# A hybrid attention layer on one core: later loads for the compressed blocks' bias, second sums one a step, masks and a value load spread out

## The chip, the cores and the metric

The kernel runs on one core of a Trainium2 chip. The metric is the device time of one execution in microseconds (us), the median of several runs.

## The reference

One decoder layer works on x of 512 x 2048 in fp32. One combined projection h = x @ w_in (11808 columns) feeds two attentions side by side and two merge gates:

```
yA  = (FoX(q, k, v, f) * silu(zA)) @ w_a          8 heads of 128
yB  = (NSA(q, 3 pairs of k/v, gates) * silu(zB)) @ w_b   8 heads, 2 groups of keys and values
out = LayerNorm(alpha * x + (sigmoid(gA)*yA + sigmoid(gB)*yB) @ w_o)
```

FoX adds c_t - c_s to its causal logits, where c is the running sum of the log forget gates; c_t drops out in the softmax, so what is added is the row of -c, masked above the diagonal. NSA mixes three branches: 31 compressed blocks (32 positions each, every 16 positions, through a small two-layer net), selected blocks and a window. Every logit of NSA gets a bias from a table of 32 distances per head; for the compressed branch this is `cbias`, one value for each position and block, masked where the block isn't past.

## The kernel before

Each fp32 product is made of three products of 32-bit "r" numbers: both operands are split into a rounded part and the rest (`split`, lines 96 to 99: ScalarE writes the rounded part, VectorE subtracts), and `mm3` (line 106) multiplies high by high, high by low and low by high. In the trace the parts of a weight are `wh` and `wl`, those of x are `xs`.

The order of the work is written out by hand. A list of units (`units`) is walked by `stream`; unit n first emits the weight split of unit n+3 (`split_w`), whose four `wh` and `wl` buffers are reused in turn, and then its own products. A dense unit has four slices of the contraction, 12 products of 512 columns; after every second slice `tick()` lets each background job advance by one step. Jobs are Python generators, a `yield` ends a step. First come those in `active` in the order of joining (loads, biases, evacuations), then the head of the queue `tq` (transposes of probabilities and products with values) and of `sq` (logits and softmax). What a step emits stands at that place in the queue of its engine, and each engine runs its queue in order; an engine that has no wait can run far ahead of the step that TensorE has reached.

The stages, in order of time:

- the transposes of x and the first projections, to about 63 us;
- `pairs`, to 561.6 us: six jobs compute 512 x 1024 pieces of the projection by sums and differences of operands (Strassen's way), seven products in each job in the order T4, T1, B11, T2, B21, T3, B22. Each has 8 units of 6 products of 512 columns, with one step after each. After T3 `out2` (line 1066) adds its result to the kept sums `c5` and `c1`, two halves each, and evacuates the four sums to DRAM by ScalarE and SyncE (`keep`, lines 1172 and 1173);
- the FoX heads, from 561.6 us: per head projections of k and q (8 units, 16 steps), with the units of the block compression between those of heads 1 to 3 and 4 to 6. `attention_open` starts three jobs, in this order in `active`: `biases`, which runs `fox_bias` for each head (GpSimd loads the row of -c to all partitions as `cbr`, and writes four masked pieces `cbx`; two `cbx` buffers, freed by `fox_s`), `raw_load` (GpSimd loads the compression's input) and `block_bias` (line 691). The last makes `cbias` as needed on chip: per head a memset of the tile `cbT` on GpSimd, a load into it from the table `fwd_d` in DRAM, four steps of waiting, then four transposes on TensorE into a `pt` bank (line 701) and a copy to `cb` on VectorE. `cb` is first read in the NSA heads, at 874 us. The value of each head is loaded by GpSimd to `vT` (one buffer) and split by `v_load`;
- the NSA heads, from about 815 us: the same with `nsa_s` and `nsa_t`. The values of a group come through the same `vT` buffer in `nsa_v_load` (line 951), first "s" (selected), then "w" (window), each three steps after its load;
- the output products and the layer norm.

Of the kernel before, what the change touches and what calls it, by code (L numbers as in the profile page):

```python
# [12 lines left out]
F32 = mybir.dt.float32  # L13
F32R = mybir.dt.float32r
AF = mybir.ActivationFunctionType
ALU = mybir.AluOpType
# [4 lines left out]
P = 128  # L21
# [24 lines left out]
PW = P * NT * (NT + 1) // 2  # L46
# [17 lines left out]
def layer(ctx, tc, x, w_in, b_f, pos_k, pos_v, wk1, wk2, wv1, wv2, w_a, w_b, w_o, ln_g, ln_b, rel, onehot, out):  # L64
    nc = tc.nc

    def dram(t, off, ap):
        return bass.AP(tensor=t.tensor, offset=t.offset + off, ap=ap)
# [22 lines left out]
    def bank(tag, bufs):  # L91
        return ps.tile([P, S], F32, name=tag, tag=tag, bufs=bufs)

    def split(hi, lo, src, scale=None):

        if scale is None:
            nc.scalar.activation(hi, src, AF.Copy)  # L97
            nc.vector.tensor_tensor(lo, src, hi.bitcast(F32), op=ALU.subtract)  # L98
        else:
            nc.scalar.activation(hi, src, AF.Copy, scale=scale)  # L100
            nc.vector.scalar_tensor_tensor(lo, src, scale, hi.bitcast(F32), op0=ALU.mult, op1=ALU.subtract)
# [13 lines left out]
    active, copies = [], []  # L115
# [148 lines left out]
    def pool(name):  # L264
        return stage[name][1]
# [14 lines left out]
    def take_later(tag):  # L280
        while free[tag] == 0:
            yield
        free[tag] -= 1
# [41 lines left out]
    def zv_rows(c0):  # L325
        return dram(zvd[:], c0, [[2 * S, P], [P * 2 * S, NT], [1, DH]])
# [48 lines left out]
    def wait_for(*keys):  # L375
        while not all(k in done for k in keys):
            yield
# [119 lines left out]
    def fox_bias(h):  # L497

        c = pool("fox").tile([P, S], F32, name="cbr", tag="cbr", bufs=2)
        nc.gpsimd.dma_start(c, dram(negc_d, h * S, [[0, P], [1, S]]))  # L500
        m = pool("fox").tile([P, PW], F32, name="cbx", tag="cbx", bufs=2)
        for i in range(NT):
            n = (i + 1) * P
            nc.gpsimd.affine_select(m[:, OFF[i]:OFF[i] + n], c[:, :n], pattern=[[-1, n]], compare_op=ALU.is_ge,
                                    fill=NEG, base=i * P, channel_multiplier=1)
        return m

    def nsa_s(h, st):
        key, g = ("n", h), h // HPG
# [115 lines left out]
    def small(name, p, n):  # L625

        return pool("hd").tile([P, S], F32, name=name, tag="om", bufs=KT)[:p, :n]
# [62 lines left out]

    def block_bias():

        for h in range(H):
            t = small("cbT", CP, S)
            nc.gpsimd.memset(t, NEG)
            nc.gpsimd.dma_start(t[:NCMP], dram(fwd_d, h * NCMP * FL + 480, [[FL - CMP_STRIDE, NCMP], [1, S]]))
            for _ in range(4):
                yield
            m = bank("pt", 2)
            for i in range(NT):  # L700
                nc.tensor.transpose(m[:, i * CP:(i + 1) * CP], t[:, i * P:(i + 1) * P], ident[:CP, :CP])
            nc.vector.tensor_copy(cb[:, h], m[:, :NT * CP].rearrange("p (i c) -> p i c", c=CP))
            yield
# [56 lines left out]
    cbxs = {}  # L760

    def biases():
        for h in range(H):
            yield from take_later("cbx")
            cbxs[h] = fox_bias(h)
            yield
            done.add(("cbx", h))

    def fox_pre(h):
# [173 lines left out]
    def nsa_v_dst(br, g):  # L943
        def f():
            assert all(("t", ("n", h)) in done for h in range(g * HPG)), "values still held"
            t = pool("nsa").tile([P, 2, NT, DH], F32R, name="nv" + br, tag="nv" + br, bufs=1)
            vt[br, g] = (t[:, 0], t[:, 1])
            return t[:, 0].rearrange("p j d -> p (j d)"), t[:, 1].rearrange("p j d -> p (j d)")
        return f

    def nsa_v_load(br, g):

        yield from take_later("vT")
        v = pool("attn").tile([P, S], F32, name="vT", tag="vT", bufs=1)
        c0 = {"s": 0, "w": S}[br] + (2 + g) * DH
        nc.gpsimd.dma_start(v.rearrange("p (j d) -> p j d", d=DH), zv_rows(c0))
        if g:
            yield from wait_for(*(("t", ("n", h)) for h in range(g * HPG)))
        for _ in range(3):
            yield  # L960
        free["vT"] += 1
        hi, lo = nsa_v_dst(br, g)()
        split(hi, lo, v)
        done.add(("v", (br, g)))

    def nsa_kv(g):
        def pre():
            if g == 0:
                nsa_open()
            for br in "sw":  # L970
                active.append(nsa_v_load(br, g))

        proj(C_KS + g * DH, evac_k(("s", g), nsa_k_dst("s", g)), pre=pre)
        proj(C_KW + g * DH, evac_k(("w", g), nsa_k_dst("w", g)))


    HT = 2

    def pairs(jobs, ops, kh, ent):

        st = {}
# [26 lines left out]
        def one(j, w, ncols, r0, cols, width, evac):  # L1008
# [55 lines left out]
                    evac(i, cols[0], st[0][i][:, :width], None)  # L1064

            def out2(width=width, cols=cols, evac=evac):
                def job():
                    for i in range(HT):
                        c5 = st["c5"][:, i, :width]
                        nc.vector.tensor_tensor(c5, st[2][i][:, :width], c5, op=ALU.add)  # L1070
                        evac(HT + i, cols[1], c5, c5)
                    yield
                    for i in range(HT):
                        c1 = st["c1"][:, i, :width]
                        nc.vector.tensor_tensor(c1, st[2][i][:, :width], c1, op=ALU.add)
                        evac(i, cols[1], c1, c1)
                g = job()
                next(g)
                active.append(g)

            def out12(width=width, cols=cols, evac=evac):
                for i in range(HT):
# [3 lines left out]
            for op, acc, fresh, quad, after, post in (  # L1086
                    ("T4", 3, True, (1, 1), first_sum, no_post), ("T1", 1, True, "s", None, keep5),
                    ("B11", 0, True, (0, 0), both_sums, keep1), ("T2", 2, True, "s", "sum4", mix),
                    ("B21", 0, False, (1, 0), None, out11), ("T3", 2, False, "r", "rest", out2),
                    ("B22", 1, False, "s", None, out12)):  # L1090
                for k in range(kh):
# [113 lines left out]
    def attention_open():  # L1205
        drain(idle)
        close_pool("sr")
        close_pool("tw")
        open_pool("hd")
        open_pool("attn")  # L1210
        open_pool("fox")
        active.append(biases())
        active.append(raw_load())
        active.append(block_bias())
# [477 lines left out]
```

## Time and profile before

| | us |
|---|---|
| three runs | 1508.80, 1506.41, 1504.27 (median 1506.41) |
| the profiled execution | 1504.97 |
| its span | 1503.2 |
| TensorE busy in it | 1481.6 (99%) |
| VectorE, ScalarE, GpSimd busy | 874.8, 668.5, 235.2 |
| mean granted clock of TensorE | 0.997 |

The span runs from the first to the last instruction of one profiled execution; that execution's own time is 1.77 us longer. Busy times of the engines overlap. A granted clock of 1.00 is 2.4 GHz and of 0.50 is 1.2 GHz. In lists of instructions "PE" is TensorE's products, "PEld" its weight loads, "DVE" VectorE, "ACT" ScalarE, "POOL" GpSimd and "SP" SyncE.

### The profile page before, as it was taken

How to read it: one execution, taken by the hardware profiler on the slowest of the kernel's cores; microseconds unless marked ns; L12 is line 12 of the kernel's file. 1: busy time of each engine (PE TensorE's matmuls, PEld its weight loads, DVE VectorE, ACT ScalarE, POOL GpSimd, SP SyncE). 2: the span in 40 equal slices, each digit the busy share in tenths (PEclk: the TensorE clock that was granted, in tenths of full speed). 3: DMA queues.
4: the chain of work that ended last, by engine and by line, in shares of the span. 5: the costliest groups of instructions: out<-in, count | busy, mean ns of one | idle time of the engine just before them, and what ended most of it. 6: DMA issues, size and time to landing. Idle time of an engine off the chain costs nothing.

```text
span 1503.2 us, 19346 instructions
## 1 busy us (share of the span) xinstructions
PE 1481.6 (99%) x6905; PEld 1220.8 (81%) x6905; DVE 874.8 (58%) x1705; ACT 668.5 (44%) x1284; POOL 235.2 (16%) x375
## 2 busy tenths in 40 slices
PE   8999999999999998999999999999999999999998
PEld 6788888888888886888888888888888888888886
DVE  4666666666666662666664466646675444444455
ACT  6255655565656562454443344434453322322233
POOL 1211230101010206545500000000000100020001
PEclk9999999999999999999999999999999999999999
DMA  8678696868686855454533322232332433362336
GB/s 229 164 227 193 185 189 195 192 190 195 191 194 185 199 145 166 122 164 120 154 113 99 104 79 71 70 91 78 92 98 89 155 114 113 123 234 98 127 112 168
DMA packets 190703, 219.05 MB, mean 146 GB/s; under 512 B 13344, under 2 KB 125008, under 8 KB 190608
## 3 DMA queue, kind: packets, MB, share of 16 engines
q1 hardware_dynamic: 164720, 160.98, 35.2%
q0 software_dynamic: 25600, 56.32, 17.4%
q8 instruction: 54, 0.88, 0.2%
q10 hardware_dynamic: 288, 0.52, 0.1%
q14 instruction: 41, 0.34, 0.1%
HBM read 199.11 MB, written 22.32 MB: 147 GB/s over the span
## 4 chain that ended last, share of the span: by engine, by line
PE 94%; DVE 2%; DMA 1%; ACT 1%; issue 1%; POOL 1%; SPq 0%; POOLq 0%; ACTq 0%; DVEq 0%
PE d L106 45%; PE s L106 17%; PE o L106 10%; PE pt L106 10%; PE m L106 8%; PE pt L417 2%; DVE wl L98 1%; PE m L112 1%; PE o L112 1%; DMA vT<-zv_d 0%; PE d L1295 0%; ACT p L399 0%; DVE xs L98 0%; DMA cbT<-fwd_d 0%; DVE p L397 0%
## 5 line engine op out<-in xcount | busy, mean ns | idle before, releaser
L98 DVE TENSOR_TENSOR wl<-wr,wh 128x512 fp32r<-128x512 f32 x460 | 317.7, 696 | 292.4 <-ACT wh L97 287.6
L97 ACT ACTIVATE wh<-wr 128x512 fp32r<-128x512 f32 x460 | 286.8, 629 | 367.5 <-PE d L106 107.9
L106 PE MATMUL d<-xs,wh 128*128 128x512 f32 x1376 | 439.6, 400 | 0.5 <-ACT xs L97 0.3
L106 PEld LDWEIGHTS d<-xs,wh 128*128 128x128 f32 x1376 | 249.6, 190 | 47.9 <-DVE xs L98 1.6
L106 PE MATMUL d<-xs,wl 128*128 128x512 f32 x688 | 270.9, 394 | 0.0
L106 PEld LDWEIGHTS d<-xs,wl 128*128 128x128 f32 x688 | 130.2, 189 | 28.9 <-DVE wl L98 0.2
L98 DVE TENSOR_TENSOR wl<-s,wh 128x512 fp32r<-128x512 f32 x144 | 98.1, 691 | 73.1 <-ACT wh L97 73.1
L97 ACT ACTIVATE wh<-s 128x512 fp32r<-128x512 f32 x144 | 89.0, 630 | 79.6 <-DVE wl L98 65.4
L106 PE MATMUL s<-wh,T 128*128 128x512 f32 x384 | 120.2, 389 | 0.0
L399 ACT ACTIVATE p<-p,mn 128x128 f32<-128x128 f32 (+3 forms) x96 | 54.0, 563 | 138.6 <-DVE mn L397 138.6
L106 PE MATMUL d<-wh,xs 128*128 128x512 f32 x336 | 111.3, 392 | 0.0
L106 PE MATMUL m<-wh,xs 128*128 128x512 f32 x256 | 99.7, 389 | 0.0
L106 PE MATMUL o<-wh,xs 128*128 128x512 f32 x240 | 93.5, 389 | 0.0
L106 PEld LDWEIGHTS s<-wh,T 128*128 128x128 f32 x384 | 72.1, 188 | 15.0
L106 PE MATMUL s<-wl,T 128*128 128x512 f32 x192 | 74.7, 389 | 0.0
L106 PEld LDWEIGHTS d<-wh,xs 128*128 128x128 f32 x336 | 63.1, 188 | 12.9
L1026 POOL DMA_DIRECT2D r<-in_w_in_dram x28 | 33.7, 1275 | 227.3 <-ACT zo L1172 178.5
L98 DVE TENSOR_TENSOR pT<-pt,pT 128x512 fp32r<-128x512 f32 (+1 forms) x96 | 46.6, 487 | 38.4 <-ACT pT L97 38.1
L106 PE MATMUL d<-wl,xs 128*128 128x512 f32 x168 | 66.2, 394 | 0.5
L841 POOL TENSOR_SCALAR af<-raw,posT 128x31 f32<-128x31 f32 x128 | 63.3, 517 | 0.3
L97 ACT ACTIVATE pT<-pt 128x512 fp32r<-128x512 f32 (+1 forms) x96 | 41.3, 431 | 44.5 <-PE pt L417 43.3
L106 PE MATMUL pt<-wh,T 128*128 128x512 f32 x192 | 60.1, 389 | 0.0
(335 smaller groups left out, 2481.5 us busy)
## 6 DMA issues: line engine op xcount, KB each, us to landing
wr<-in_w_in_dram SPq DMA_DIRECT2D x147, 512.0 KB, 3.8
wr<-in_w_o_dram SPq DMA_DIRECT2D x32, 512.0 KB, 3.7
r<-in_w_in_dram SPq DMA_DIRECT2D x20, 512.0 KB, 4.7
r<-in_w_in_dram POOLq DMA_DIRECT2D x20, 512.0 KB, 10.7
s<-in_w_in_dram POOLq DMA_DIRECT2D x20, 512.0 KB, 6.6
wr<-in_w_a_dram SPq DMA_DIRECT2D x16, 512.0 KB, 3.7
wr<-in_w_b_dram SPq DMA_DIRECT2D x16, 512.0 KB, 3.7
wr<-in_w_in_dram SPq DMA_DIRECT2D x26, 256.0 KB, 3.4
```

What stands on the lines that cost most here:

```text
L97: nc.scalar.activation(hi, src, AF.Copy)
L98: nc.vector.tensor_tensor(lo, src, hi.bitcast(F32), op=ALU.subtract)
L106: nc.tensor.matmul(o, u, v, start=first and n == 0, stop=last and n == 2, **kw)
L112: nc.tensor.matmul(*u, start=first and u is whole, stop=last and u is whole)
L399: nc.scalar.activation(row, row, AF.Exp, bias=it["mn"][:, i:i + 1], scale=-1.0, accum_out=it["l"][:, i:i + 1])
L417: nc.tensor.transpose(b[:, (i - j) * P:(i - j + 1) * P], pt[:, OFF[i] + j * P:OFF[i] + (j + 1) * P], ident)
L841: nc.gpsimd.tensor_scalar(af[:, l, g], src, posT[:, po0 + ll:po0 + ll + 1], None, op0=ALU.add)
L1026: nc.gpsimd.dma_start(st[n][:, k - 1:k + 1, part], src, accum_op=ALU.add)
```

## The change

`block_bias` waits 24 steps before its first head, and eight steps in place of four between load and use. `fox_bias` is made a generator: after the load of `cbr` it waits four steps, then for a free `cbx` buffer, and writes one masked piece a step; `biases` runs it and marks the head as done behind the last. `nsa_v_load` waits six steps for the window values, three for the selected ones. `out2` no longer runs its first half at once and its second in the same unit's step: each step does one addition and evacuates the sum of the step before.

```diff
@@ fox_bias @@
         nc.gpsimd.dma_start(c, dram(negc_d, h * S, [[0, P], [1, S]]))
-        m = pool("fox").tile([P, PW], F32, name="cbx", tag="cbx", bufs=2)
+        for _ in range(4):
+            yield
+        yield from take_later("cbx")
+        cbxs[h] = m = pool("fox").tile([P, PW], F32, name="cbx", tag="cbx", bufs=2)
         for i in range(NT):
             n = (i + 1) * P
             nc.gpsimd.affine_select(m[:, OFF[i]:OFF[i] + n], c[:, :n], pattern=[[-1, n]], compare_op=ALU.is_ge,
                                     fill=NEG, base=i * P, channel_multiplier=1)
-        return m
+            yield
@@ block_bias @@
+        for _ in range(24):
+            yield
         for h in range(H):
             t = small("cbT", CP, S)
             nc.gpsimd.memset(t, NEG)
             nc.gpsimd.dma_start(t[:NCMP], dram(fwd_d, h * NCMP * FL + 480, [[FL - CMP_STRIDE, NCMP], [1, S]]))
-            for _ in range(4):
+            for _ in range(8):
                 yield
@@ biases @@
         for h in range(H):
-            yield from take_later("cbx")
-            cbxs[h] = fox_bias(h)
-            yield
+            yield from fox_bias(h)
             done.add(("cbx", h))
@@ nsa_v_load @@
-        for _ in range(3):
+        for _ in range(3 if br == "s" else 6):
             yield
@@ out2 @@
                 def job():
-                    for i in range(HT):
-                        c5 = st["c5"][:, i, :width]
-                        nc.vector.tensor_tensor(c5, st[2][i][:, :width], c5, op=ALU.add)
-                        evac(HT + i, cols[1], c5, c5)
-                    yield
-                    for i in range(HT):
-                        c1 = st["c1"][:, i, :width]
-                        nc.vector.tensor_tensor(c1, st[2][i][:, :width], c1, op=ALU.add)
-                        evac(i, cols[1], c1, c1)
-                g = job()
-                next(g)
-                active.append(g)
+                    todo = None
+                    for n, i0 in (("c5", HT), ("c1", 0)):
+                        for i in range(HT):
+                            c = st[n][:, i, :width]
+                            nc.vector.tensor_tensor(c, st[2][i][:, :width], c, op=ALU.add)
+                            if todo:
+                                evac(*todo)
+                            todo = i0 + i, cols[1], c, c
+                            yield
+                    evac(*todo)
+                active.append(job())
```

## Rows read from the trace of the kernel before

**Rows 1.** The page: busy time, share of the span and instructions of each engine.
```profile
PE 1481.6 (99%) x6905; PEld 1220.8 (81%) x6905; DVE 874.8 (58%) x1705; ACT 668.5 (44%) x1284; POOL 235.2 (16%) x375
```
**Rows 2.** Waits of TensorE's products: engine, line, awaited, total us, times, longest us.
```profile
PE pt L701 <- DMA cbT<-fwd_d: 3.8, 1, 3.8
PE pt L701 <- issue: 2.6, 1, 2.6
...
PE s L106 <- ACT q L100: 1.0, 1, 1.0
```
**Rows 3.** Waits of TensorE's weight loads, same columns.
```profile
PEld d L106 <- DVE wl L98: 3.3, 7, 0.5
...
PEld pt L417 <- DVE cb L702: 0.3, 1, 0.3
```
**Rows 4.** The chain that ended last: start us, us, what and how many.
```profile
539.42 10.88 PE s L106 x48
550.30 3.63 PE d L106 x16
...
553.95 0.70 DVE wl L98
...
554.69 6.91 PE d L106 x29
```
**Rows 5.** Timeline of GpSimd: start, us, engine, line, operation, count, [idle before <- releaser].
```profile
566.34 1.12 POOL L808 DMA_DIRECT2D raw<-raw_dk  x2 [3.17 <-DMA sig_d<-zo]
...
568.16 0.55 POOL L695 MEMSET cbT<- 32x512 f32 x1
569.00 0.54 POOL L696 DMA_DIRECT2D cbT<-fwd_d  x1 [0.29 <-POOL cbT L695]
569.53 0.78 POOL L339 DMA_DIRECT2D vT<-v_d  x1
...
575.42 1.73 POOL L504 TENSOR_SCALAR_AFFINE_SELECT cbx<-cbr 128x128 f32<-128x128 f32 x4 [4.04 <-DMA cbr<-negc_d]
...
579.73 0.53 POOL L696 DMA_DIRECT2D cbT<-fwd_d  x1 [0.29 <-POOL cbT L695]
```
**Rows 6.** Timeline of TensorE's products around line 701.
```profile
571.31 0.40 PE L701 MATMUL pt<-ident,cbT 32*128 32x32 f32 x4 [2.62 <-issue]
...
584.18 0.40 PE L701 MATMUL pt<-ident,cbT 32*128 32x32 f32 x4 [3.84 <-DMA cbT<-fwd_d]
```
**Rows 7.** The eight loads of the tile cbT, from issue to landing.
```profile
DMA to landing us min/median/max: 2.0/2.4/4.3
```
**Rows 8.** Windows: length, busy us (count) per engine, granted clock, DMA share, GB/s.
```profile
571.75:575.10 3.35, 3.35 (x8) 2.68 (x9) 1.57 (x4) 1.79 (x3) 0.00 (x0) 0.50 0.61 202
...
585.35:588.70 3.35, 3.35 (x10) 2.58 (x9) 0.16 (x1) 0.00 (x0) 3.22 (x7) 0.50 0.39 111
```
**Rows 9.** Timeline of ScalarE at the first head's value.
```profile
572.86 0.63 ACT L97 ACTIVATE v<-vT 128x512 fp32r<-128x512 f32 x1 [7.82 <-DMA vT<-v_d]
573.40 1.37 ACT L97 ACTIVATE wh<-wr 128x512 fp32r<-128x512 f32 x2
```
**Rows 10.** Timeline of ScalarE and VectorE after the last job's T3.
```profile
550.97 2.42 ACT L1172 ACTIVATE c<-c 128x512 f32<-128x512 f32 x4 [1.36 <-DVE c L1070]
551.45 1.28 DVE L1075 TENSOR_TENSOR c<-s,c 128x512 f32<-128x512 f32 x2
...
553.30 2.18 ACT L97 ACTIVATE wh<-s 128x512 fp32r<-128x512 f32 x4
```
**Rows 11.** Timeline of TensorE's products and ScalarE at the second group's window value.
```profile
1014.58 0.39 PE L106 MATMUL d<-xs,wl 128*128 128x512 f32 x1
1014.83 0.63 ACT L97 ACTIVATE nvw<-vT 128x512 fp32r<-128x512 f32 x1 [4.86 <-DMA vT<-zv_d]
...
1017.09 0.62 PE L106 MATMUL d<-xs,wh 128*128 128x512 f32 x2
```
**Rows 12.** Timeline of GpSimd in head 4.
```profile
695.27 0.78 POOL L339 DMA_DIRECT2D vT<-v_d  x1 [15.05 <-DVE r L404]
```

## The prediction

> **What bounds the kernel now.** The page's table of engines comes first: TensorE is busy for 1481.6 of 1503.2 us [rows 1]. So the change can only win what TensorE loses: 21.6 us of idle time, and whatever it runs slowly. Work taken off another engine is worth nothing by itself. The next view is therefore what TensorE waited for [rows 2]. Of its waits, two belong to line 701, the transposes of the compressed blocks' bias (2.6 us, put down to "issue", and 3.8 us for the load of `cbT`), and one to ScalarE's `q` (1.0 us). The reader should see that these are a few single stops, not a steady loss, and that the other parts of the change must show elsewhere: in TensorE's weight loads (waits of up to 0.5 us, seven times, on VectorE's `wl` [rows 3]) and in the rows of time around each stop.
>
> I count a step as half a unit of a projection. 48 products of 512 columns take 10.88 us [rows 4], 0.227 us each; a step of six is 1.36 us and a unit of twelve 2.72 us.
>
> **Part 1, the bias of the compressed blocks.** Before, the first load is issued in step 1 and used in step 5. The order on GpSimd shows why four steps don't do at the start [rows 5]: its loads of `raw` wait until 566.34 for stores of the stage before, so the first `cbT` load goes out at 569.00, while TensorE arrives there at 568.7 and stands for 2.62 us [rows 6]. The second load stands behind the mask of head 1, which waits 4.04 us for its own `cbr` load (575.42); it goes out at 579.73, as TensorE is about to use it, and lands 4.3 us later, the longest of the eight [rows 7]. TensorE starts again at 584.18, 3.84 us late [rows 6].
>
> Each stop is paid twice. After it the granted clock is 0.50 (the level of 1.2 GHz) for a stretch, with TensorE busy throughout: 3.35 us from 571.75 and 3.35 us from 585.35 [rows 8]. Half of such a stretch is lost, 1.68 us. So the stops cost 2.62 + 1.68 + 3.84 + 1.68 = 9.82 us.
>
> After: the first load goes out in step 25 and is used in step 33, each further one nine steps later, the last in step 96; all of it lies in heads 1 to 5 (a head is 16 steps, 18 to 19 with compression units). At use a load has had 8 x 1.36 = 10.9 us. It needs the memset and the issue (about 1.4 us, 568.16 to 569.53 [rows 5]) and at most 4.3 us of landing [rows 7], so up to 5.2 us of delay on GpSimd is covered. What can stand ahead of it there: masks that wait for VectorE's use of the old mask, `vT` loads that wait for the split of the value before, and up to eight additions of the compression. The two waits end by about the step in which the blocked instruction was written, since what they wait for was written a step or two earlier. I take nothing for the eight places; the bounds are 0 (six of the eight had no stop at four steps) and 5.52 us each, the second stop with its clock. The transposes themselves are moved, not removed.
>
> The transposes use the `pt` banks, which the heads' transposes use too. Head 3's fall in steps 83 to 87 and one bias transpose in step 87; the one such meeting in the trace of before cost a weight load 0.3 us [rows 3], so 0 to 0.3, and I take 0.
>
> What is late next, once TensorE doesn't stop: ScalarE stands at the split of head 0's value until 572.86, when `vT` lands, 3.33 us after its issue at 569.53 [rows 5, 9]. Without the memset and load ahead of it, `vT` goes out at 568.16 and lands near 571.5. The weights behind it then have both halves 1.9 us later (split of the value 0.54, of the weight 0.69 on ScalarE and 0.70 on VectorE [rows 4, 9]), at 573.4. TensorE, undisturbed, wants them after five units: 561.6 + 13.6 = 575.2. That cover is 1.8 us; a later `vT` costs what it exceeds that.
>
> **Part 2, the masks of the heads.** `cbr` is loaded at least four steps before its first mask, and the four masks go one a step. GpSimd no longer stands for `cbr` (4.04 us in the row above), and nothing on TensorE's path waits: head 0's mask is done in step 9 and used from step 18, and each later one still has most of a head. Nothing for itself; it clears the queue for part 1 and the values.
>
> **Part 3, the second sums of the split products.** Before, a job's four additions run back to back on VectorE (two pairs of 1.28 us) and ScalarE evacuates them in 2.42 us; four weight splits then crowd behind, the first ending too late [rows 10]. In the chain the stretch of 48 products that starts at 550.30 holds VectorE's `wl` at 553.95 and ends at 561.60: 11.30 us against 10.88 [rows 4]. There are six jobs and the chain has the same piece in each: 0.4 us each, 2.4 us. After, a unit has one addition (0.64) and one split (0.70) on VectorE, 1.34 us against TensorE's 1.36. That is tight, but three units are split ahead and it lasts four units, ending before the next job's first sums. Bounds: 0 to 2.4 gained; I take 2.4. The stores are issued up to four steps later, after which SyncE has no weight load due until the sixth unit, so none is held up.
>
> **Part 4, the window value.** At 1009.97 ScalarE reaches the split of `nvw`, and stands 4.86 us until its load lands. Behind it is the split of `q`, whose projection ended two steps before its use, near 1012.1. TensorE wants `q` at 1014.8, gets its first half late and its second later still, and takes up projections at 1017.09 [rows 2, 11]. From the last product at 1014.58, 0.23 + 3 x 0.14 (320 of 512 columns) would bring that to 1015.23, so 1.86 us are lost. With six steps the `nvw` split comes three steps later in ScalarE's order, behind `q` and behind the landing; what waits for it, the head's second products, is many steps off. In the first group no such wait shows. I take 1.86; bounds 0 and 1.86.
>
> **Sum.** 9.82 + 2.4 + 1.86 = 14.1 us. The profiled run took 1504.97 us, 1.77 of them outside the span, and would take 1490.9. It is 1.44 us under the median of the three runs, which I take for scatter; from the median 1506.41 the forecast is 1492.3 us.
>
> **The rivals**, all from that median.
>
> *The sums gain nothing:* VectorE at 1.34 of 1.36 us is the bound in those units, and six waits of 0.4 us stay. For it: the margin of 0.02. Against: three units of lead. 1494.7 us.
>
> *The stop moves:* TensorE, no longer halted, catches up with ScalarE at head 0's value, because `vT` lands some 4 us later than I reckon. For it: all loads of that start wait for one store (566.34). Against: `vT` is earlier in the queue than now. At the price of the first stop, 4.3 us: 1496.6 us.
>
> *It does not do what it says:* the two stops come back at other `cbT` uses, or TensorE is held by something that the stops hide. Only parts 3 and 4 gain, 4.3 us: 1502.1 us.
>
> *Slower:* the loads, now in the busiest stretch of GpSimd, stand behind its long waits for VectorE (the `vT` load at 695.27 came after 15.05 us [rows 12]) and land after their use. Each then costs 5.52 us, the second stop again; eight are 44.2, and the time 1536. It decides from the third of the eight (14.1 / 5.52 = 2.6). Against it: those waits are GpSimd running ahead of the others, and end at about the step in which they were written; six loads at four steps made no stop. The Trainium skill, "SBUF — State Buffer", section "SBUF: two separate sides", holds for this side too: VectorE in certain operations locks GpSimd out of a port it needs to write the descriptors of its loads, and a load of 620 ns took 3100 beside one. By that page, as an estimate, a landing would grow by 2.5 us; alone it stays inside the 5.2 us of cover, and needs a queue of 2.7 us besides to stop TensorE. The trace shows no starved issue: those of `cbT` take 0.53 and 0.54 us in the rows.
>
> **How the numbers follow.** Forecast 0.70 (own range 1489 to 1495, the scatter of the runs and the collision), sums without gain 0.10, a moved stop 0.10, not doing what it says 0.06, slower 0.04. The likeliest gives 1492.3. The range 1488 to 1500 takes in the first three and leaves out about a tenth, and a little of the forecast's tails. A measurement of this kernel tells about 0.3%, 4.5 us, from no change: the first three cases lie well beyond it, the fourth just inside. Faster 0.90, within 0.06, slower 0.04.
>
> **What would show it.** In the profile after: no wait of TensorE on line 701, and a granted clock of 1.00 from 562 to 640 us (part 1); no 4 us wait of GpSimd for `cbr` (part 2); the products after each job's second sums in 10.88 us (part 3); `q` ahead of `nvw` on ScalarE and no wait for `q` (part 4). TensorE's idle time would fall from 21.6 to about 14 us. I am wrong if line 701 waits in heads 1 to 5, or if TensorE stops between 570 and 580 for weights held up by `vT`.

## The result, and the profile after

The changed kernel takes 1492.67 us (median of six runs, 1492.17 to 1493.58) where the kernel before takes 1505.80 beside it (six runs, 1502.51 to 1508.80): ratio 0.9916, 95% interval 0.9906 to 0.9927. Forecast were 1492.3 us and a range of 1488 to 1500. So it is faster, by 0.8%, about as much as forecast; but one term of the sum turns out to belong to the one profiled run and not to the kernel, as the experiments show.

The profiled run took 1492.17 us, its span 1490.0. TensorE's line of the page, and its longest waits (engine, line, awaited, total us, times, longest us):

```profile
PE 1477.0 (99%) x6905; PEld 1219.3 (82%) x6905; DVE 878.1 (59%) x1705; ACT 670.4 (45%) x1284; POOL 236.0 (16%) x375
```

```profile
PE s L1599 <- DMA xa<-in_x_dram: 4.5, 1, 4.5
PE pt L417 <- DVE pT L98: 0.6, 1, 0.6
PE s L106 <- DVE mn L397: 0.5, 1, 0.5
...
PE pt L706 <- issue: 0.2, 1, 0.2
```

The two stops at the bias transposes (line 701 before, 706 now) [rows 2, 6] are gone, and so is the wait for `q`. The largest left is the load of x at the very start. TensorE's idle time is 1490.0 - 1477.0 = 13.0 us; 14 were forecast.

**Part 1.** The loads of `cbT` on GpSimd and their uses on TensorE, two of eight (third and seventh), with the landings of all:

```profile
625.14 0.55 POOL L701 DMA_DIRECT2D cbT<-fwd_d  x1 [0.29 <-POOL cbT L700]
...
685.83 0.56 POOL L701 DMA_DIRECT2D cbT<-fwd_d  x1 [0.29 <-POOL cbT L700]
```

```profile
639.05 0.43 PE L706 MATMUL pt<-ident,cbT 32*128 32x32 f32 x4
...
699.73 0.40 PE L706 MATMUL pt<-ident,cbT 32*128 32x32 f32 x4 [0.16 <-issue]
```

```profile
DMA to landing us min/median/max: 2.1/3.0/4.0
```

From issue to use there are 13.9 us in both, the least of the eight, against a landing of at most 4.0. The use at 699.73 is the one that meets head 3's transposes: it costs 0.16 us there. The granted clock (windows: length, busy us and count for PE, PEld, DVE, ACT, POOL, then the clock) is now 1.00 where two stretches stood at 0.50 [rows 8]:

```profile
560.00:640.00 80.00, 79.34 (x398) 65.67 (x398) 44.97 (x101) 36.02 (x82) 54.17 (x104) 1.00 0.59 175
640.00:720.00 80.00, 79.84 (x411) 65.78 (x411) 49.43 (x125) 35.15 (x84) 37.36 (x72) 1.00 0.45 133
```

**Part 3.** In the chain the stretch behind the last second sums takes 10.88 us, with no wait of VectorE in it [rows 4]; so do the other five. On VectorE (second fence) an addition and a split alternate, the additions 1.36 us apart, and neither shows a wait:

```profile
548.59 10.88 PE d L106 x48
559.48 14.36 PE d L106 x62
573.87 10.74 PE d L106 x46
```

```profile
548.54 0.69 DVE L1076 TENSOR_TENSOR c<-s,c 128x512 f32<-128x512 f32 x1
549.29 0.69 DVE L98 TENSOR_TENSOR wl<-s,wh 128x512 fp32r<-128x512 f32 x1
549.90 0.68 DVE L1076 TENSOR_TENSOR c<-s,c 128x512 f32<-128x512 f32 x1
550.70 0.69 DVE L98 TENSOR_TENSOR wl<-s,wh 128x512 fp32r<-128x512 f32 x1
```

The third row of the chain is the place of the "moved stop": it begins 0.03 us late at 573.87, where the weights behind head 0's value come. ScalarE got the value at 571.81 and not at 571.5; its load took 4.7 us (issued at 567.07) and not 3.3 [rows 9]. The cover of 1.8 us that I had reckoned was used up; comparing the starts of the next products, TensorE lost 0.3 us.

```profile
571.81 0.63 ACT L97 ACTIVATE v<-vT 128x512 fp32r<-128x512 f32 x1 [8.88 <-DMA vT<-v_d]
572.35 1.14 ACT L97 ACTIVATE wh<-wr 128x512 fp32r<-128x512 f32 x2
```

**Part 4.** `q` now stands ahead of `nvw` on ScalarE, and TensorE goes through the products that had waited [rows 11] in 0.44 us:

```profile
1000.02 0.60 ACT L100 ACTIVATE q<-d 128x512 fp32r<-128x512 f32 x1 [2.31 <-PE d L106]
1003.06 0.62 ACT L97 ACTIVATE nvw<-vT 128x512 fp32r<-128x512 f32 x1
```

```profile
1002.55 0.60 PE L106 MATMUL s<-nk,q 128*128 128x320 f32 x3
1002.99 0.39 PE L106 MATMUL d<-xs,wh 128*128 128x512 f32 x1
```

**Where the span's 13.2 us went**, by the start of the same product in the two traces. The products of the FoX stage begin at 559.48 and not at 561.60: 2.1 us (part 3 gave 2.4, the first projections began 0.3 later). Its last logits show what the heads gave; first the kernel before, then after:

```profile
829.34 0.86 PE L106 MATMUL s<-k,q 128*128 128x512 f32 x3
```

```profile
817.07 0.86 PE L106 MATMUL s<-k,q 128*128 128x512 f32 x3
```

That is 12.3, so 10.2 in the heads: 9.1 at the bias and 1.1 from two waits in head 4 (for `a` and for `z`) that are shorter in this run. At 1002.99 against 1017.09 [rows 11] it is 14.1, so 1.8 more are won at the window value. These are not part 4's doing: the same products win 1.7 to 1.9 us on the trace of before in four traces that keep the old three steps (the bias alone, the sums alone and the two smaller kernels below), because the window value's load landed late in the trace of before and in none of these. Of the 14.1, 0.9 are given back in small pieces up to the end; 0.2 of them some 8 us on, which the trace with the value's six steps alone loses there too and the four with three steps don't.

### The profile page after: what moved, and what is told of

It is laid out like the page before. It is cut to its first block, busy times and chain, and to the rows that moved or that the text cites. A ratio compares the mean times of both kernels' runs of the same rounds, so it can differ in the third digit from the quotient of the medians.

```text
span 1490.0 us, 19352 instructions
## 1 busy us (share of the span) xinstructions
PE 1477.0 (99%) x6905; PEld 1219.3 (82%) x6905; DVE 878.1 (59%) x1705; ACT 670.4 (45%) x1284; POOL 236.0 (16%) x375
## 4 chain that ended last, share of the span: by engine, by line
PE 97%; DVE 2%; ACT 1%; issue 0%; DMA 0%; SPq 0%; ACTq 0%
PE d L106 47%; PE s L106 17%; PE o L106 10%; PE pt L106 10%; PE m L106 8%; PE pt L417 2%; PE m L112 1%; PE o L112 1%; PE d L1298 0%; DVE wl L98 0%; ACT p L399 0%; DVE xs L98 0%; DVE p L397 0%; DMA wr<-in_w_in_dram 0%; PE s L1599 0%
```

## The experiments

Times are medians; ratios are to the kernel before, run in turn with them on the same chip, with 95% intervals. Where a ratio is turned into us, it is of the kernel before's 1504.2.

**One part alone.** Before, with the bias part only: `for _ in range(24): yield` ahead, and

```diff
-            for _ in range(4):
+            for _ in range(8):
```

> The kernel before with the bias part alone: 24 steps ahead of the first head, eight between load and use. Theory (the parts add, the bias is the main one): both stops at the transposes go, with their two stretches at half clock; 9.1 us less than before (what the two traces show between the end of the split products and the last use of the bias), no wait on the transposes, granted clock 1.00 from 560 to 720 us. Rival (the masks' part is needed to clear GpSimd's queue): GpSimd still stands about 4 us for each row of -c, the loads come late in heads 1 to 5, and less than 5 us is won.

1494.18 us, ratio 0.9937 (0.9922 to 0.9951): 9.5 us less. No wait at the transposes but one of 0.27 us at the meeting with head 3's; no stretch at half clock. The masks are not needed for it. The rival falls.

With the masks' part only (`fox_bias` as a generator, as in the change):

> The kernel before with the masks' part alone. Theory (the second stop comes from the mask of head 1, which stands in front of the second load until its row of -c lands): the second load goes out some 5 us earlier, so the second stop goes and its half-clock stretch with it, 5.5 us less than before; the first stop of about 2.6 us and its stretch at half clock stay, because the first load waits for stores of the stage before. Rival (my prediction took this part for nothing by itself; the stop is the four steps' alone): both stops stay and the time is that of before within 1 us.

1500.61 us, 0.9973 (0.9961 to 0.9984): 4.1 us less (2.4 to 5.9), where I had predicted nothing for this part by itself; the rival falls. GpSimd, then TensorE's first transposes:

```profile
569.72 0.53 POOL L699 DMA_DIRECT2D cbT<-fwd_d  x1 [0.29 <-POOL cbT L698]
...
574.74 0.55 POOL L699 DMA_DIRECT2D cbT<-fwd_d  x1 [0.29 <-POOL cbT L698]
```

```profile
572.21 0.40 PE L704 MATMUL pt<-ident,cbT 32*128 32x32 f32 x4 [2.98 <-issue]
581.16 0.43 PE L704 MATMUL pt<-ident,cbT 32*128 32x32 f32 x4
```

The second load goes out at 574.74 and not at 579.73 [rows 5], and the second stop is gone; the first stays, with 2.98 us. So the two stops have two causes: the second the mask of head 1, the first, as GpSimd's wait for the store reads [rows 5], the stores of the stage before; that one was not tested apart. The bias part removes both, the masks' part the second, and so the gains don't add.

With the second sums only:

> The kernel before with the second sums one a step, alone. Theory: six waits of 0.4 us go, each stretch of 48 products behind the sums takes 10.88 us in the chain and not 11.28; 2.4 us less than before. Rival (VectorE at 1.34 of 1.36 us bounds these units, or the stores issued later hold up the next stage's first loads): 0 to 1 us less, with a wait on VectorE's or SyncE's row later in the same stage or at its end.

1500.25 us, 0.9977 (0.9966 to 0.9989): 3.5 us less, with 2.4 inside the interval (1.7 to 5.1). In its trace each of the six stretches is 0.4 us shorter, the last below, and nothing waits later. The rival falls. Its twelve runs lie in two groups (seven from 1498.5 to 1500.7 us, five from 1503.2 to 1506.0), so the size is better read from the trace than from the median.

```profile
549.72 10.89 PE d L106 x48
```

With the window value's six steps only:

```diff
-        for _ in range(3):
+        for _ in range(3 if br == "s" else 6):
```

> The kernel before with the window value's six steps alone. Theory: ScalarE splits q before it meets the value that has not landed; no wait of TensorE for q in the second group; 1.7 to 1.9 us less than before. Rival (the wait only moves, to the weights behind the value on ScalarE): a wait of TensorE on weights some units later, and 0 to 0.5 us less.

1505.09 us, 0.9999 (0.9987 to 1.0010): no gain to be seen, though the times alone leave room for up to 2.0 us. The wait for `q` is gone from the trace, and the products run as in the changed kernel; but the load took 3.9 us in this trace, and with such a landing there is no wait to remove. Neither theory foresaw that. It shows in the other traces that have the old three steps. The landing of this one load (window 990 to 1025 us), in the kernel before, with the masks alone and with the sums alone:

```profile
DMA to landing us min/median/max: 5.9/5.9/5.9
```

```profile
DMA to landing us min/median/max: 5.0/5.0/5.0
```

```profile
DMA to landing us min/median/max: 3.9/3.9/3.9
```

It landed after 4.0 us with the bias alone, and after 4.0 and 4.2 us in the two smaller kernels below. Where it took 3.9 to 4.2 us, ScalarE still stood for it (2.8 to 3.1 us), but `q` was ready in time and TensorE didn't wait; with 5.0 us it lost 0.9 us, with 5.9 us 1.8. The stop that I had priced was that of a run with a late load.

**Which of the two numbers of the bias part does it.** The changed kernel without the 24 steps:

> The changed kernel with the 24 steps taken out, the eight steps kept: the bias begins at once, as before. Theory (the late start is needed for the queue, not for the bias: the first load and its memset, 1.4 us, stand in front of the first head's value, whose cover is used up in the changed kernel): the value lands about 1.4 us later than 571.8, ScalarE frees the weights at about 575.1 where TensorE wants them at 573.5, so TensorE stops for 1.2 to 2 us for weights (not at the transposes), with or without a stretch at half clock: 1.2 to 4 us slower than the changed kernel. Rival (the eight steps alone do it): no stop anywhere, within 0.5 us of the changed kernel. Second rival (a load at the start needs more than eight steps): a stop at the first transposes again, 2 to 4 us slower.

1491.85 us, 0.9917 (0.9903 to 0.9930): no slower than the changed kernel. My theory falls. The load of `cbT` does stand ahead of the value, but the value landed 3.4 us after its issue (4.7 in the changed kernel), so ScalarE had it at 571.32. This is no accident of one run, as the last section shows. TensorE has no wait for these weights; one of 0.8 us stands where a head's transposes meet a piece of the bias. GpSimd, then ScalarE:

```profile
567.35 0.53 POOL L699 DMA_DIRECT2D cbT<-fwd_d  x1 [0.29 <-POOL cbT L698]
567.86 0.79 POOL L339 DMA_DIRECT2D vT<-v_d  x1
```

```profile
571.32 0.63 ACT L97 ACTIVATE v<-vT 128x512 fp32r<-128x512 f32 x1 [8.67 <-DMA vT<-v_d]
```

The changed kernel with four steps in place of eight, the late start kept:

> The changed kernel with four steps between load and use in place of eight, the late start kept. Theory (behind step 24 GpSimd runs ahead of TensorE, so that the loads are issued 14 to 22 us before use at eight steps and still 8 us or more at four): no wait at the transposes, within 0.5 us of the changed kernel. Rival (in the busiest stretch of GpSimd the loads come late, as in my slower case): three or more of the eight stop TensorE, at 3 to 5.5 us each, 10 us slower or more.

1493.34 us, 0.9928 (0.9916 to 0.9941): no wait at the transposes. In its trace other waits of 0.4 to 1.4 us at the heads' transposes and at `a` are longer than in the changed kernel's first profile (the longest, for `z`, is 1.2 us in its second). So with the masks' part there, either number is enough by itself. Eight steps are enough without the masks too, as the smallest change below shows; the late start with four steps was not run without them.

With one step between load and use, and eight behind the use:

```diff
-            for _ in range(8):
+            for _ in range(1):
                 yield
...
-            yield
+            for _ in range(8):
+                yield
```

> The changed kernel with one step between load and use and eight more behind the use, so that each load is emitted in the same step as in the changed kernel. Theory (issue to use was 13.9 to 21.8 us, less seven steps of 1.36 is 4.4 to 12.3 us, and landings took 2.1 to 4.0): no stop or two of at most 0.5 us, within 1 us of the changed kernel. Rival (the slower case of my prediction: each late load costs 5.5 us): most of the eight stop TensorE, 20 to 44 us slower.

1494.44 us, 0.9932 (0.9919 to 0.9946), less than 2 us above the changed kernel. One of eight uses stops, for 0.93 us (I had expected 0.5 at most), and the clock behind it stays at 1.00:

```profile
628.05 0.40 PE L706 MATMUL pt<-ident,cbT 32*128 32x32 f32 x4 [0.93 <-DMA cbT<-fwd_d]
```

```profile
628.50:632.00 3.50, 3.50 (x23) 3.13 (x24) 3.50 (x8) 2.24 (x6) 3.50 (x6) 1.00 0.56 155
```

Its load went out behind a mask that had waited 2.47 us for VectorE:

```profile
624.78 0.29 POOL L507 TENSOR_SCALAR_AFFINE_SELECT cbx<-cbr 128x128 f32<-128x128 f32 x1 [2.47 <-DVE mn L397]
...
625.83 0.55 POOL L701 DMA_DIRECT2D cbT<-fwd_d  x1 [0.29 <-POOL cbT L700]
```

The eight loads went out 2.2 to 8.9 us before their use, where I had reckoned 4.4 to 12.3. So what the slower case describes does happen, but once in eight and for 0.93 us, not 5.52: in heads 1 to 5 GpSimd is ahead of TensorE by itself, even with one step.

**Less queue in front of the value.** `raw_load` begins two steps later, and the bias after 25 steps and not 24:

```diff
     def raw_load():
+        for _ in range(2):
+            yield
```

> The changed kernel with the loads of the compression's input two steps later, so that the first head's value goes out ahead of them, and with 25 in place of 24 steps ahead of the bias, so that no transposes of it fall in a step with those of a head. Theory: the value lands 2 us earlier or more, the loss of about 0.3 us at the weights behind it goes, and the 0.2 us at the bias transposes that met head 3's go too: 0.5 us less than the changed kernel, which the times can hardly tell but the waits can. Rival: the loads moved back come late for the compression or another meeting takes the place of that one; 0 to 2 us slower.

1492.39 us, 0.9919 (0.9906 to 0.9933), not to be told from the changed kernel by its time. The mechanism is as expected: the value goes out at 565.48 and is there at 568.78, TensorE has no wait for these weights, and no wait at a bias transpose is left; the span is 1489.2 us.

```profile
565.48 0.76 POOL L339 DMA_DIRECT2D vT<-v_d  x1 [7.79 <-DMA sig_d<-zo]
```

```profile
568.78 0.63 ACT L97 ACTIVATE v<-vT 128x512 fp32r<-128x512 f32 x1 [5.36 <-DMA vT<-v_d]
```

**The smallest change that does it**, run beside the changed kernel. First the bias part and the sums, without masks and value:

> The kernel before with the bias part and the sums alone, without the masks' and the window value's parts. Theory (the bias alone won 0.63%, the sums 2.4 us by their trace, and the other two nothing that is left once the bias is late): within 1 us of the changed kernel run beside it; TensorE's wait for q in the second group may show or not, as the value's load lands. Rival (the masks' 4 us or the value's 1.9 us come on top): 2 us or more slower than the changed kernel.

1492.09 us, 0.9919 (0.9905 to 0.9932). Then eight steps and the sums, the bias begun at once, masks and value as before:

> The kernel before with eight steps in place of four between load and use, begun at once, and the sums; masks and value as before. Theory (eight steps cover the first load, which is issued near 568 and wanted near 572, but the second stands behind head 1's mask, is issued near 579 and wanted near 584, so that its 2 to 4.5 us of landing just do): no stop over 1 us at the transposes, within 2 us of the changed kernel. Rival (without the masks' part or the late start the second load still comes late): one stop of 1 to 3 us with its stretch at half clock, 3 to 5 us slower than the changed kernel.

1492.87 us, 0.9921 (0.9908 to 0.9935). The second load is indeed late, but eight steps cover it: issued at 580.14, used at 586.04, neither use with a stop.

```profile
575.32 2.27 POOL L504 TENSOR_SCALAR_AFFINE_SELECT cbx<-cbr 128x128 f32<-128x128 f32 x4 [3.69 <-DMA cbr<-negc_d]
...
580.14 0.53 POOL L696 DMA_DIRECT2D cbT<-fwd_d  x1 [0.29 <-POOL cbT L695]
```

```profile
573.22 0.43 PE L701 MATMUL pt<-ident,cbT 32*128 32x32 f32 x4
586.04 0.43 PE L701 MATMUL pt<-ident,cbT 32*128 32x32 f32 x4
```

The changed kernel itself, on that chip:

> The changed kernel again, beside the other two on the same chip. All theories: 1492 to 1494 us, the runs within 2 us of each other, since no stop of variable length is left; the kernel before within 6 to 8 us of itself.

1493.88 us (1493.44 to 1494.57), 0.9929 (0.9917 to 0.9942). Both smaller versions are not slower than it. The five runs with two parts (1491.16 to 1492.82) all lie below its five; 1.8 us is 0.12%, the two traces differ in pieces of up to 0.5 us in several stages, and I claim no cause for it. The kernel before ranged from 1502.9 to 1506.7 in that session.

## Why the prediction was right, and where not

*Part 1* was right in mechanism and nearly in size: 9.82 us forecast, 9.5 measured alone, 9.1 in the two traces. The transposes at the new places cost nothing more, as the landings of at most 4.0 us and the 13.9 us of issue to use show; the meeting in step 87 cost 0.16 us of TensorE's time (0 to 0.3 forecast). That each stop is paid twice also held: behind the seven stops of 2.4 to 4.3 us at these transposes, in the four traces that have any, the granted clock fell to 0.50, and where the stops are gone it stays at 1.00. The Trainium skill, "TensorE: Matmul & The Clock Gate", section "What's actually happening", gives the same two levels.

*Part 2* was wrong as an isolated statement: it is worth 4.1 us without part 1, because the second stop hung on the mask of head 1. Beside part 1 no worth of it shows (two parts: 0.9919, all four: 0.9916 and 0.9929), which is all that the sum needed.

*Part 3* was right: 2.4 forecast, six times 0.4 in the traces, 3.5 (1.7 to 5.1) by the times. VectorE at 1.34 of 1.36 us was no bound.

*Part 4* failed as a term: 1.86 us forecast, no gain measured (-1.5 to 2.0, which by itself does not rule the 1.86 out). The step that failed is the one from the row to the kernel: "1.86 us are lost" holds for one execution, in which the load took 5.9 us. Of the six traces with three steps one lost 1.8 us, one 0.9 and four nothing, which makes 0.5 us on average, an estimate from these six; the kernel's value lies near my lower bound, 0.

*The cover*, 1.8 us at head 0's value, was used up, for two reasons. I had counted TensorE's five units from 561.6, but part 3 of the same sum brings that start to 559.48, so that TensorE wants the weights at 573.1 and not 575.2. And the load, with nothing of the bias ahead of it, took 4.7 us, and 5.3 in the changed kernel's second profile, not the 3.3 of the one row that I had. The rival of a moved stop was real, at 0.3 us instead of 4.3.

*The total* came out closer than its terms, and that is luck. Without part 4 the sum is 12.2 us; the ratios of the changed kernel give 12.6 and 10.7. And the 1506.41 us that I subtracted from, a median of three runs, lay 2.2 above the 1504.22 of the 24 runs later on. The forecast of 1492.3 had a gain of about 2 us too many taken from a start of about 2 us too high.

*The slower case* rested on a real row, a wait of 15 us on GpSimd [rows 12], but that wait is GpSimd's lead over the others: it is there in the changed kernel too (15.10 us), and with one step between load and use seven of eight loads still landed in time. The port lock of the Trainium skill ("SBUF — State Buffer", "SBUF: two separate sides") does not show at these loads: in the changed kernel the issues of `cbT` take 0.54 to 0.57 us and the loads land after 4.0 us at most. Whether it lies behind the longest landing here, 5.9 us, no run shows.

## What to carry to other kernels

Where one engine is busy for 99%, list its stops one by one, price each by the rows around it with the slower clock behind it, and ask which queue made it: two neighbouring stops here had different causes, and one edit removed both. A stop that hangs on the landing of one load is a draw, not a constant; before it goes into a sum, compare the load's landing with those of its like. And a long wait on an engine that runs ahead (GpSimd's 15 us) is first of all a lead; how little distance the loads behind it need can be tried, as here with one step: one of eight came late, by 0.93 us.

## What the runs showed that was not expected

One load of 256 KB, the same instruction at the same place (the window value), landed after 3.7 to 4.2 us in eleven of the thirteen traces, after 5.0 us in one and after 5.9 in one, that of the kernel before. What lengthens it in one run isn't settled.

Head 0's value is another case, and goes with the kernel. It landed after 3.2 to 3.4 us in the six traces in which the bias begins at once and in the one in which `raw_load` begins two steps later, and after 4.1 to 5.3 us in the six others, in which it goes out straight behind the loads of the compression's input. In the twelve traces that have these loads ahead of it, ScalarE began on the value 6.0 to 7.2 us after the first of them went out, whether the memset and load of `cbT` stood between or not. The prediction had reckoned that with the bias out of the way the value would land earlier; counted from these loads it didn't. With `raw_load` out of the way it did (568.78). Why its landing goes with these loads, no run shows.

In the changed kernel, without these stops, most of the scatter is gone. The 24 runs of the kernel before beside the single parts span 8.0 us (1499.62 to 1507.61); the eleven of the changed kernel span 2.4 us (1492.17 to 1494.57) over two sessions. The lengths of the stops don't account for all of it: the two measured 2.4 and 3.4 us in one trace (the window value alone) and 3.3 and 4.3 in another (the sums alone), 1.8 us apart in sum. The clock goes with part of it: of the 24 runs, the ten with a mean granted clock of 0.995 have a median of 1504.88 us, the three with 0.998 one of 1501.95. The rest stays open, as does one run of the bias part alone, 1499.02 us where its other five lie between 1493.29 and 1495.12.
